# Two layers of fp32r matmuls on one core: finer start loads, spaced x loads, one seven-product quad fewer, and SBUF tiles at multiples of 512 bytes

## The chip, the cores and the metric

The kernel runs on one core of a Trainium2 chip. The time is the device time of one execution in microseconds; the figure of a kernel is the median of its runs. Before the change it is 2428.97 us (three runs, 2428.86 to 2429.07).

## The reference

A decoder trunk of two layers on 256 tokens of width 2048, in fp32. Layer 0 is a retention layer with 8 heads, layer 1 multi-head latent attention over a shared, compressed key and value; each is followed by an MLP with squared ReLU and 8192 hidden columns. The two MLPs hold most of the weights and are what the change mostly touches:

```
for layer in range(2):
    x = x + (retention if layer == 0 else mla)(rms_norm(x, norm_mix[layer]), ...)
    h = rms_norm(x, norm_mlp[layer])
    x = x + square(relu(h @ w1[layer])) @ w2[layer]     # 2048 -> 8192 -> 2048
```

## The kernel before, in words

**The product.** Every weight is read once, as fp32, by 1 MB loads on SyncE's (SP's) DMA queue into four `raw` buffers. A product of fp32 numbers is three fp32r matmuls: ScalarE (ACT) casts the high part `wh` of a weight, VectorE (DVE) subtracts it from `raw` and leaves the low part `wl` (`split`, L695), and TensorE (PE) does high by high, high by low and low by high. The last of these subtractions that was recorded is kept in `low_part[0]`.

**Quads.** The unit of the large products is `quad` (L826): two blocks of 128 rows of a weight by two of 512 columns, times both halves of the tokens. An ordinary quad has 8 products, 24 matmuls of 128x128 by 512 columns. A "seven" quad has 7 products, 21 matmuls, in Strassen's manner: DVE first makes sums of blocks of the weight (`u0`, `u1`; one addition over 1024 elements and two over 512), and four parts instead of two are split into `wh` and `wl`, seven half parts in place of four. `gemm_pair` (L882) does eight quads that sum into one set of PSUM banks; `kinds` says which of the eight are of the seven kind. L527 names sets of them: `SEVEN` (3, 5, 7), `LATE` (5, 7), `ODD` (1, 3, 5, 7).

**The MLP** (`mlp`, L1348) goes through the 8192 hidden columns in four groups. A group has two up pairs (p = 0 and 1 in the first group, to p = 6 and 7 in the last), which make eight hidden blocks, and then two down pairs, which use them. `u{layer}_{p}{quad}` names an up quad's tiles, `d{layer}_{group}{p}{quad}` a down quad's. A hidden block goes from PSUM through sums on DVE and ReLU on ACT, is cut into two 16-bit halves by copies (`hid_h`), turned by DMA transposes on SP's queue (`hid_t`, four for a half pair), copied together (`hid_u`), squared and split into `hid` on ACT and DVE, with sums `hid_more` for the seven quads. In profile names the numbers are left out: `u_wl`, `d_c`, `hid_t`.

**The residual stream** x lies in device memory (`xh`). At the end of each of four products (retention output, MLP 0, attention output, MLP 1) `x_tiles` (L622) brings it in: four blocks, two loads of 256 KB each, on GpSimd's (POOL's) queue. `later(n, f)` (L579) puts a step off by n quads, and `tick` (L587) counts them; so the code is recorded in an order in which, for example, block b of x is brought when 2b quads more have been recorded.

**The order of the work.** The engines do not run the code as recorded. `Plan` (L126) keeps every instruction as an `Op` with a table cost; `latest` (L256) goes backwards and gives each a due date; `forward` (L313) places them engine by engine, the earliest due date first among those that are ready by the plan; `schedule` (L293) repeats this six times and keeps the plan with the earliest end. `emit` (L469) writes the result out, so that nearly every instruction has the line L480 in the profile. Once written, each engine and each queue goes through its list strictly in order. `behind(op, other)` (L226) makes op wait for other. All SBUF tiles of a tag rotate through fixed slots; the first tiles of the program (`gains`, 448 bytes on each partition, `cst`, `inv`, 640 bytes) lie ahead of the pools of large tiles.

**The start.** `gemm_two` (L816) makes the first two projections (q and k of a head) together from `rq_raw`, half of which is loaded after the other, with the first loads of x transposed (`x0t`) between; `a0` is x times the norm's gain, one half of it by ACT and one by DVE. PE runs 11 idle matmuls on zeros until then.

Of the kernel before, what the change touches and what calls it, by code (L numbers as in the profile page):

```python
# [120 lines left out]
class Op:  # L121
    __slots__ = ("engine", "method", "args", "kw", "number", "before", "after", "cost", "took", "due", "start", "end",
                 "new", "left", "ready", "made", "held", "moves", "behind", "ahead")


class Plan:  # L126
# [19 lines left out]
    def record(self, engine, method, args, kw):  # L146
# [3 lines left out]
        op.made = op.held = None  # L150
# [105 lines left out]
    def latest(self):  # L256
# [4 lines left out]
        limit, free = {}, dict.fromkeys(self.LATENCY, 0.0)  # L261
# [8 lines left out]
        while True:  # L270
# [12 lines left out]
            op.due = free[e] = min(limit[op], free[e] - op.cost)  # L283
# [29 lines left out]
    def forward(self):  # L313
# [73 lines left out]
        while True:  # L387
            best = None
            for e in free:
                w, r = waiting[e], ready[e]  # L390
                while w and w[0][0] <= free[e]:
                    _, _, op = heapq.heappop(w)
                    heapq.heappush(r, (op.due, op.number, op))
# [11 lines left out]
            if not ready[e]:  # L405
                while waiting[e] and waiting[e][0][0] <= at:
                    _, _, op = heapq.heappop(waiting[e])
                    heapq.heappush(ready[e], (op.due, op.number, op))
# [102 lines left out]
P = 128  # L511
# [36 lines left out]
def yoco(ctx: ExitStack, tc: tile.TileContext, a):  # L548
# [48 lines left out]
    gains = nc.tile(pool, [P, G_ALL + 14], F32, "gains")  # L597
    cst = nc.tile(pool, [P, C_ALL - C_MASK], F32, "cst")
    inv = nc.tile(pool, [P, C_MASK], F32, "inv")
# [22 lines left out]
    def x_tiles(name):  # L622


        def bring(b):
            both = act_tile(f"x_{name}{b}", F32)
            for t in range(NT):
                x[t][b] = both[:, t].rearrange("p i s -> p (i s)")
                nc.gpsimd.dma_start(x[t][b], x_home[t][b])

        for b in range(NB):
            later(2 * b, lambda b=b: bring(b))
# [112 lines left out]
    def stream(w, chunk, cols, name, use, done=None, before=None):  # L745

        raw = nc.tile(pool, [P, 2048], F32, f"{name}_raw", "raw", 4)
        if before is None:
            nc.sync.dma_start(raw[:, :cols], w[chunk])
        n = cols // 2  # L750
        for half in range(2):
            wh = nc.tile(pool, [P, 1024], F32R, f"{name}_wh{half}", "wh", 5)
            wl = nc.tile(pool, [P, 1024], F32R, f"{name}_wl{half}", "wl", 5)
            cuts = 1
            if before is not None:
                cuts = 1 if half or chunk else 2
                m = n // cuts
                for i in range(cuts):
                    lo = half * n + i * m
                    nc.sync.dma_start(raw[:, lo : lo + m], w[chunk][:, lo : lo + m])  # L760
                    if i == 0:
                        before(half)
            m = n // cuts
            for i in range(cuts):
                lo = half * n + i * m
                low_part[0] = split(wh[:, i * m : (i + 1) * m], wl[:, i * m : (i + 1) * m], raw[:, lo : lo + m])
# [21 lines left out]
    def four_t(acc, act, k0, nk, wh, wl):  # L788

        for j in range(4):  # L790
# [25 lines left out]
    def gemm_two(w, act, nk, names, before, done):  # L816
# [3 lines left out]
        for g in range(n):  # L820
            stream(
                w, g, 2048, f"{names[0]}{g}", lambda half, wh, wl: four_t(acc[half], act, g * 4, nk, wh, wl),
# [989 lines left out]
```

## Time and profile before

| | |
|---|---|
| median of three runs | 2428.97 us (2428.86 to 2429.07) |
| the profiled execution, its time and its span | 2431.72 us, 2429.9 us |
| mean granted clock of TensorE | 0.996 |
| busy: PE, PEld, DVE, ACT, POOL | 2405.2, 2013.8, 2262.6, 1852.3, 219.2 us |
| their shares of the span | 99, 83, 93, 76, 9% |
| matmuls recorded | 11190 |
| bytes moved by DMA | 545.18 MB, 224 GB/s |

The profile shows one execution. PE are matmuls, PEld the loading of their stationary operand, DVE VectorE, ACT ScalarE, POOL GpSimd; SPq and POOLq are the DMA queues of SP and POOL. A row of a timeline has the start and the length in us, the engine, the operation with its tiles (out<-in, partitions x elements) and the count; in brackets stands how long the engine was idle before it, and what ended that. A row of the waits has engine and tile, what it waited for, and the total, the times and the longest in us. A group has busy time and mean ns of one, then the idle time before them. A row of a table by windows has the stretch, its length, and the busy time of PE, PEld, DVE, ACT and POOL with counts, then PEclk, the granted clock as a share of full speed, the busy share of the DMA engines, and GB/s. Times of one instruction from row to row are read from starts, since the ends of matmuls are modelled.

### The profile page before, as it was taken

To read this page: it belongs to the slowest core of one execution; us is meant where nothing else is said; L and a number is where in the kernel's file an instruction comes from. 1 tells how busy PE (TensorE), PEld (TensorE's weight loads), DVE (VectorE), ACT (ScalarE), POOL (GpSimd) and SP (SyncE) were. 2 spreads that over 40 slices of the span, in tenths; PEclk is the share of its full clock that TensorE was granted. 3 is DMA by queue.
4 is the path that set the end of the run, shared out by engine and by line. 5 is a ranking of instruction groups with operands and counts; after the bars stand their busy time and mean duration, and the time that the engine had idled before them with its cause. 6 is when DMAs were issued, how large, how long until landed. Compare 5 with 4: busy or idle time off the path is not lost. (4 is left out here: it accounts for less than half of the span.)

```text
span 2429.9 us, 31583 instructions
## 1 busy us (share of the span) xinstructions
PE 2405.2 (99%) x11190; PEld 2013.8 (83%) x11190; DVE 2262.6 (93%) x3002; ACT 1852.3 (76%) x2613; POOL 219.2 (9%) x245
## 2 busy tenths in 40 slices
PE   9999999999999999999999999999999999999999
PEld 7888888888887788888877888998887888888877
DVE  8999999989999999999989998877899999999989
ACT  7666766667787969769769979677879688697795
POOL 3000001011000010010110001110000100100100
PEclk9999999999999999999999999999999999999999
DMA  8566669667585698799897766545767997987974
GB/s 339 191 203 210 204 210 256 201 200 237 200 260 189 220 271 228 242 262 231 239 269 223 217 226 190 169 145 188 220 208 215 257 238 233 258 240 243 265 235 145
DMA packets 197136, 545.18 MB, mean 224 GB/s; under 512 B 115441, under 2 KB 116977, under 8 KB 143729
## 3 DMA queue, kind: packets, MB, share of 16 engines
q1 hardware_dynamic: 174720, 495.84, 63.5%
q0 software_dynamic: 21248, 46.15, 9.9%
q8 instruction: 87, 1.43, 0.2%
q10 hardware_dynamic: 1008, 1.18, 0.2%
q14 instruction: 73, 0.59, 0.1%
HBM read 478.09 MB, written 39.85 MB: 213 GB/s over the span
## 5 line engine op out<-in xcount | busy, mean ns | idle before, releaser
L480 PE MATMUL d_c<-d_wh,hid 128*128 128x512 f32 x1412 | 455.1, 391 | 4.2 <-ACT hid L480 4.2
L480 PE MATMUL u_c<-u_wh,n 128*128 128x512 f32 x1328 | 428.9, 390 | 3.1 <-ACT u_wh L480 3.1
L480 PEld LDWEIGHTS d_c<-d_wh,hid 128*128 128x128 f32 x1412 | 266.5, 189 | 61.4 <-ACT hid L480 5.0
L480 PEld LDWEIGHTS u_c<-u_wh,n 128*128 128x128 f32 x1328 | 249.7, 188 | 55.3 <-ACT u_wh L480 3.8
L480 DVE TENSOR_TENSOR d_wl<-d_raw,d_wh 128x1024 fp32r<-128x1024 f32 (+1 forms) x256 | 279.2, 1108 | 5.4 <-ACT d_wh L480 5.4
L480 ACT CAST u_wh<-u_raw 128x1024 fp32r<-128x1024 f32 (+1 forms) x256 | 235.9, 952 | 62.5 <-PE u_c L480 49.1
L480 DVE TENSOR_TENSOR u_wl<-u_raw,u_wh 128x1024 fp32r<-128x1024 f32 (+1 forms) x256 | 272.6, 1095 | 8.9 <-ACT u_wh L480 8.6
L480 PE MATMUL d_c<-d_wl,hid 128*128 128x512 f32 x706 | 275.8, 391 | 0.1
L480 ACT CAST d_wh<-d_raw 128x1024 fp32r<-128x1024 f32 (+1 forms) x256 | 240.4, 964 | 40.7 <-PE d_c L480 23.2
L480 PE MATMUL u_c<-u_wl,n 128*128 128x512 f32 x664 | 259.4, 391 | 3.1 <-DVE u_wl L480 3.1
L480 PE MATMUL rp_c<-rp_wh,a 128*128 128x512 f32 x640 | 206.6, 390 | 0.0
L480 ACT CAST rp_wh<-rp_raw 128x1024 fp32r<-128x1024 f32 (+1 forms) x128 | 118.4, 944 | 65.6 <-PE rp_c L480 36.7
L480 DVE TENSOR_TENSOR u_wl<-u_u,u_wh 128x1024 fp32r<-128x1024 f32 x120 | 145.3, 1220 | 22.3 <-ACT u_wh L480 21.6
L480 ACT CAST d_wh<-d_u 128x1024 fp32r<-128x1024 f32 x106 | 108.8, 1052 | 69.4 <-DVE d_u L480 59.6
L480 ACT CAST u_wh<-u_u 128x1024 fp32r<-128x1024 f32 x120 | 125.4, 1052 | 43.2 <-PE u_c L480 19.4
L480 PEld LDWEIGHTS d_c<-d_wl,hid 128*128 128x128 f32 x706 | 133.2, 189 | 28.2 <-DVE d_wl L480 0.5
L480 PEld LDWEIGHTS u_c<-u_wl,n 128*128 128x128 f32 x664 | 124.7, 188 | 32.4 <-DVE u_wl L480 6.6
L480 DVE TENSOR_TENSOR rp_wl<-rp_raw,rp_wh 128x1024 fp32r<-128x1024 f32 (+1 forms) x128 | 136.1, 1092 | 8.6 <-ACT rp_wh L480 7.8
L480 PEld LDWEIGHTS rp_c<-rp_wh,a 128*128 128x128 f32 x640 | 120.1, 188 | 26.0 <-DVE rk_u L480 0.9
L480 DVE TENSOR_TENSOR d_wl<-d_u,d_wh 128x1024 fp32r<-128x1024 f32 x106 | 127.6, 1220 | 5.9 <-ACT d_wh L480 5.6
L480 PE MATMUL u_p<-u_wh,n_more 128*128 128x512 f32 x360 | 122.7, 395 | 2.2 <-ACT u_wh L480 2.2
L480 PE MATMUL rp_c<-rp_wl,a 128*128 128x512 f32 x320 | 124.5, 389 | 0.0
(464 smaller groups left out, 5941.4 us busy)
## 6 DMA issues: line engine op xcount, KB each, us to landing
u_raw<-in_mlp_w SPq DMA_DIRECT2D x128, 1024.0 KB, 6.3
d_raw<-in_mlp_w SPq DMA_DIRECT2D x128, 1024.0 KB, 5.3
rp_raw<-in_ret_w_gv SPq DMA_DIRECT2D x64, 1024.0 KB, 5.0
ro_raw<-in_ret_w_out SPq DMA_DIRECT2D x32, 1024.0 KB, 5.1
uq_raw<-in_mla_w_uq SPq DMA_DIRECT2D x24, 768.0 KB, 4.2
rq_raw<-in_ret_w_qk SPq DMA_DIRECT2D x14, 1024.0 KB, 5.7
rk_raw<-in_ret_w_qk SPq DMA_DIRECT2D x14, 1024.0 KB, 5.3
xh<-d_c POOLq DMA_DIRECT2D x48, 256.0 KB, 5.5
```

The source lines that it names most:

```text
L480: op.made = fn(*(real(v) for v in op.args), **{k: real(v) for k, v in op.kw.items()})
```

## The change

There are four parts. (1) *Start:* the first group of the two first projections is loaded in four pieces of 512 columns, q and k by turns, and an op can carry a `first`, a place ahead of all due dates, which fixes the order of these loads and of the first x loads on SP; the cast of the positions goes from DVE to POOL. (2) *x loads and due dates:* `latest` lets the transfers of all queues share one server when it works out due dates, and each x load is recorded by itself, one per quad, from one quad later on, and waits for the last low-part subtraction recorded by then. (3) *Kinds of quads:* up pair p = 1 of both layers has the set (3, 5, 7) of seven quads in place of (1, 3, 5, 7): its quad 1 becomes ordinary. (4) *Addresses:* `gains` grows from 448 to 896 bytes per partition, and `inv` moves into a 2048-byte `f2k` slot. Before, the `raw` buffers began 64 bytes, and the other large tiles 192 bytes, past a multiple of 512; after, all begin at multiples of 512.

```diff
@@ -120,7 +120,7 @@
     __slots__ = ("engine", "method", "args", "kw", "number", "before", "after", "cost", "took", "due", "start", "end",
-                 "new", "left", "ready", "made", "held", "moves", "behind", "ahead")
+                 "new", "left", "ready", "made", "held", "moves", "behind", "ahead", "first")
@@ -147,7 +147,7 @@
         op.number, op.before, op.after, op.new = len(self.ops), {}, [], []
-        op.made = op.held = None
+        op.made = op.held = op.first = None
         op.behind, op.ahead = set(), []
@@ -258,7 +258,7 @@
         behind = {op: [] for op in self.ops}
-        limit, free = {}, dict.fromkeys(self.LATENCY, 0.0)
+        limit, free, server = {}, dict.fromkeys(self.LATENCY, 0.0), 0.0
         waiting = {e: [] for e in free}
@@ -280,7 +280,11 @@
             op = heapq.heappop(ready[e])[2] if ready[e] else heapq.heappop(waiting[e])[3]
-            op.due = free[e] = min(limit[op], free[e] - op.cost)
+            op.due = min(limit[op], free[e] - op.cost)
+            if op.moves is not None:
+                server = min(server, op.due + op.cost + op.moves[0]) - op.moves[0]
+                op.due = min(op.due, server - op.cost)
+            free[e] = op.due
             for other, finish in behind[op]:
@@ -390,7 +394,7 @@
                     _, _, op = heapq.heappop(w)
-                    heapq.heappush(r, (op.due, op.number, op))
+                    heapq.heappush(r, (op.due if op.first is None else op.first - 1e9, op.number, op))
                 at = free[e] if r else w[0][0] if w else None
@@ -405,7 +409,7 @@
                     _, _, op = heapq.heappop(waiting[e])
-                    heapq.heappush(ready[e], (op.due, op.number, op))
+                    heapq.heappush(ready[e], (op.due if op.first is None else op.first - 1e9, op.number, op))
             _, _, op = heapq.heappop(ready[e])
@@ -594,9 +598,9 @@
-    gains = nc.tile(pool, [P, G_ALL + 14], F32, "gains")
+    gains = nc.tile(pool, [P, G_ALL + 126], F32, "gains")
     cst = nc.tile(pool, [P, C_ALL - C_MASK], F32, "cst")
-    inv = nc.tile(pool, [P, C_MASK], F32, "inv")
+    inv = f2k([C_MASK], "inv")
     pos_i = nc.tile(few, [P, NT], I32, "pos_i")
@@ -626,10 +630,14 @@
                 x[t][b] = both[:, t].rearrange("p i s -> p (i s)")
-                nc.gpsimd.dma_start(x[t][b], x_home[t][b])
+                def load(dst=x[t][b], src=x_home[t][b]):
+                    nc.behind(nc.gpsimd.dma_start(dst, src), low_part[0])
+                later(t, load)
         for b in range(NB):
-            later(2 * b, lambda b=b: bring(b))
+            later(2 * b + 1, lambda b=b: bring(b))
@@ -742,28 +750,15 @@
-    def stream(w, chunk, cols, name, use, done=None, before=None):
+    def stream(w, chunk, cols, name, use, done=None):
         raw = nc.tile(pool, [P, 2048], F32, f"{name}_raw", "raw", 4)
-        if before is None:
-            nc.sync.dma_start(raw[:, :cols], w[chunk])
+        nc.sync.dma_start(raw[:, :cols], w[chunk])
         n = cols // 2
             wl = nc.tile(pool, [P, 1024], F32R, f"{name}_wl{half}", "wl", 5)
-            cuts = 1
-            if before is not None:
-                cuts = 1 if half or chunk else 2
-                m = n // cuts
-                for i in range(cuts):
-                    lo = half * n + i * m
-                    nc.sync.dma_start(raw[:, lo : lo + m], w[chunk][:, lo : lo + m])
-                    if i == 0:
-                        before(half)
-            m = n // cuts
-            for i in range(cuts):
-                lo = half * n + i * m
-                low_part[0] = split(wh[:, i * m : (i + 1) * m], wl[:, i * m : (i + 1) * m], raw[:, lo : lo + m])
+            low_part[0] = split(wh[:, :n], wl[:, :n], raw[:, half * n : half * n + n])
             use(half, wh, wl)
@@ -785,9 +780,9 @@
-    def four_t(acc, act, k0, nk, wh, wl):
-        for j in range(4):
+    def four_t(acc, act, k0, nk, wh, wl, js=range(4)):
+        for j in js:
             k = k0 + j
@@ -818,10 +813,28 @@
         for g in range(n):
-            stream(
-                w, g, 2048, f"{names[0]}{g}", lambda half, wh, wl: four_t(acc[half], act, g * 4, nk, wh, wl),
-                (lambda: done(acc)) if g == n - 1 else None, lambda half: before(g) if half == 0 else None,
-            )
+            raw = nc.tile(pool, [P, 2048], F32, f"{names[0]}{g}_raw", "raw", 4)
+            parts = [
+                [nc.tile(pool, [P, 1024], F32R, f"{names[0]}{g}_{i}{half}", i, 5) for i in ("wh", "wl")] for half in range(2)
+            ]
+            cuts = 1 if g else 2
+            m = 1024 // cuts
+            for i in range(cuts):
+                for half in range(2):
+                    lo = half * 1024 + i * m
+                    ins = nc.sync.dma_start(raw[:, lo : lo + m], w[g][:, lo : lo + m])
+                    if not g:
+                        ins.first = (0, 3, 4, 6)[2 * i + half]
+                    if half == i == 0:
+                        before(g)
+                    wh, wl = parts[half]
+                    low_part[0] = split(wh[:, i * m : (i + 1) * m], wl[:, i * m : (i + 1) * m], raw[:, lo : lo + m])
+            for i in range(cuts):
+                for half in range(2):
+                    four_t(acc[half], act, g * 4, nk, *parts[half], range(i * 4 // cuts, (i + 1) * 4 // cuts))
+            if g == n - 1:
+                queue.append((clock[0] + 0.5, -1, lambda: done(acc)))
+            tick()
@@ -1124,7 +1137,7 @@
     def first_tables():
-        nc.vector.tensor_copy(pos_f, pos_i)
+        nc.gpsimd.tensor_copy(pos_f, pos_i)
         turned_by.append(sincos(inv, C_MASK, "tab"))
@@ -1148,10 +1161,12 @@
         if c:
-            nc.sync.dma_start(t, a["xt"][:, 2 * c : 2 * c + 2, :])
+            ins = nc.sync.dma_start(t, a["xt"][:, 2 * c : 2 * c + 2, :])
+            if c == 1:
+                ins.first = 5
         else:
             for j in range(2):
-                nc.sync.dma_start(t[:, j], a["xt"][:, j, :])
+                nc.sync.dma_start(t[:, j], a["xt"][:, j, :]).first = 1 + j
         v = act_tile(f"a0_{c}")
@@ -1396,7 +1411,7 @@
             for p in range(f0 // 2, (f0 + nf) // 2):
-                seven = (ODD, ODD)[p % 2] if p else LATE
+                seven = (LATE, SEVEN, *(ODD, ODD) * 3)[p]
                 gemm_pair(
```

What the plan makes of it is shown at three places. First SP's list in layer 0, second up pair: `u0_16_raw` is the load of its quad 6, `hid0_00` the first hidden block pair of the first up pair (t0, t1 its two turned halves, h0 and h1 the 16-bit halves), `d0_000_raw` the first load of the down pair. Before:

```order
L480 DMA u0_15_raw_7116<-in_mlp_w1_0 128x2048
L480 DMA u0_17_raw_7197<-in_mlp_w1_0 128x2048
L480 DMA_TRANSPOSE hid0_00_t0_7212<-hid0_00_h0_7201 128x4x128
L480 DMA_TRANSPOSE hid0_00_t1_7222<-hid0_00_h0_7201 128x4x128
L480 DMA u0_16_raw_7236<-in_mlp_w1_0 128x2048
L480 DMA_TRANSPOSE hid0_00_t0_7212<-hid0_00_h1_7240 128x4x128
L480 DMA_TRANSPOSE hid0_00_t1_7222<-hid0_00_h1_7240 128x4x128
L480 DMA d0_000_raw_7291<-in_mlp_w2_0 128x2048
L480 DMA d0_001_raw_7312<-in_mlp_w2_0 128x2048
L480 DMA_TRANSPOSE hid0_01_t0_7374<-hid0_01_h0_7364 128x4x128
```

After, the same place:

```order
L484 DMA u0_15_raw_7143<-in_mlp_w1_0 128x2048
L484 DMA_TRANSPOSE hid0_00_t0_7166<-hid0_00_h0_7154 128x4x128
L484 DMA_TRANSPOSE hid0_00_t0_7166<-hid0_00_h1_7162 128x4x128
L484 DMA_TRANSPOSE hid0_00_t1_7189<-hid0_00_h0_7154 128x4x128
L484 DMA_TRANSPOSE hid0_00_t1_7189<-hid0_00_h1_7162 128x4x128
L484 DMA u0_17_raw_7211<-in_mlp_w1_0 128x2048
L484 DMA_TRANSPOSE hid0_01_t0_7217<-hid0_01_h0_7187 128x4x128
L484 DMA_TRANSPOSE hid0_01_t0_7217<-hid0_01_h1_7215 128x4x128
L484 DMA u0_16_raw_7239<-in_mlp_w1_0 128x2048
L484 DMA_TRANSPOSE hid0_01_t1_7243<-hid0_01_h0_7187 128x4x128
L484 DMA_TRANSPOSE hid0_01_t1_7243<-hid0_01_h1_7215 128x4x128
L484 DMA d0_000_raw_7310<-in_mlp_w2_0 128x2048
```

All four transposes of the first block pair now stand ahead of the load of quad 7, and those of the second ahead of the first load of the down pair.

Second, POOL's list at the x loads of MLP 0, with the semaphores that each load waits for (PE, DVE: that engine; DMASW: an earlier transfer of POOL's queue); `xh_0_1` is block 1 of x for the first half of the tokens. Before:

```order
L480 DMA x_mlp00_11555<-xh_0_0_455 128x512 [waits PE_49]
L480 DMA x_mlp00_11555<-xh_1_0_470 128x512
L480 DMA x_mlp01_11574<-xh_0_1_505 128x512 [waits PE_49]
L480 DMA x_mlp01_11574<-xh_1_1_514 128x512
L480 DMA x_mlp02_11590<-xh_0_2_525 128x512 [waits DMASW4_49,PE_49]
L480 DMA x_mlp02_11590<-xh_1_2_538 128x512 [waits DMASW5_49]
```

After:

```order
L484 DMA x_mlp00_11942<-xh_0_0_459 128x512 [waits DVE_49]
L484 DMA x_mlp00_11942<-xh_1_0_497 128x512 [waits DVE_49]
L484 DMA x_mlp01_12053<-xh_0_1_511 128x512 [waits DVE_49]
L484 DMA x_mlp01_12053<-xh_1_1_520 128x512 [waits DVE_49]
L484 DMA x_mlp02_12209<-xh_0_2_530 128x512 [waits DMASW4_49,DVE_49]
L484 DMA x_mlp02_12209<-xh_1_2_543 128x512 [waits DMASW5_49,DVE_49]
```

Each load waits for a subtraction of DVE of its own. The number at a tile's end counts what was recorded: the loads were recorded together, 11555 to 11668 with the fourth block, as the last up pair ended, and now stand apart, from 11942 on, beside the eight quads of the down pair after it.

Third, DVE's list at the start (`gqn` is a gain, `pos_f` the positions as floats, `rq00_wl` a low part of the first projections' weights, `a0_0` their other operand). Before:

```order
L480 TENSOR_SCALAR gqn_99<-gains_68 128x1
L480 CAST pos_f_111<-pos_i_78 128x2
L480 TENSOR_TENSOR rq00_wl0_118<-rq00_raw_74,rq00_wh0_108 128x512
L480 SCALAR_TENSOR_TENSOR a0_0_120<-x0t_0_80,gains_68,a0_0_120 128x256
L480 TENSOR_TENSOR rq00_wl0_118<-rq00_raw_74,rq00_wh0_108 128x512
L480 TENSOR_TENSOR rq00_wl1_155<-rq00_raw_74,rq00_wh1_148 128x1024
```

After:

```order
L484 TENSOR_SCALAR gqn_98<-gains_68 128x1
L484 TENSOR_TENSOR rq00_wl0_117<-rq00_raw_74,rq00_wh0_107 128x512
L484 SCALAR_TENSOR_TENSOR a0_0_119<-x0t_0_80,gains_68,a0_0_119 128x256 x2
L484 TENSOR_TENSOR rq00_wl1_144<-rq00_raw_74,rq00_wh1_132 128x512
L484 TENSOR_TENSOR rq00_wl0_117<-rq00_raw_74,rq00_wh0_107 128x512
```

The cast of the positions is gone from DVE, both halves of `a0` stand together, and the k half (`wl1`) comes between the two pieces of the q half.

## The prediction, on record before the changed kernel was run

> **What bounds the kernel now.** I read the page's first lines, then who TensorE (PE) waited for, then the stretches around those waits.
>
> ```profile
> span 2429.9 us, 31583 instructions
> PE 2405.2 (99%) x11190; PEld 2013.8 (83%) x11190; DVE 2262.6 (93%) x3002; ACT 1852.3 (76%) x2613; POOL 219.2 (9%) x245
> ```
>
> PE is busy 99% of the span: the floor is the matmuls themselves, and an edit can win only what PE waits, or a cheaper matmul. The waits of PE, all of them that matter here (us in total, times, longest):
>
> ```profile
> PE d_c L480 <- ACT hid L480: 4.2, 2, 2.4
> PE u_c L480 <- ACT u_wh L480: 3.1, 1, 3.1
> PE u_c L480 <- DVE u_wl L480: 3.1, 5, 0.8
> PE u_p L480 <- ACT u_wh L480: 2.2, 1, 2.2
> PE rq_acc L480 <- DVE a L480: 1.8, 1, 1.8
> PE u_p L480 <- DVE u_wl L480: 1.4, 2, 0.8
> ...
> PE d_c L480 <- DVE hid_more L480: 0.3, 1, 0.3
> PE rp_p L480 <- ACT rp_wh L480: 0.2, 1, 0.2
> ```
>
> They sit in three kinds of place: the start (rq_acc), the second up-projection pair of each layer and the down-projection after it, and the last up-projection pair of each layer. The same view cut to the second pair and what follows, in layer 0 (754 to 830 us) and in layer 1 (1795 to 1870 us), gives the shares:
>
> ```profile
> PE u_c L480 <- DVE u_wl L480: 0.7, 1, 0.7
> PE u_p L480 <- DVE u_wl L480: 0.6, 1, 0.6
> ```
> ```profile
> PE u_c L480 <- DVE u_wl L480: 1.4, 2, 0.8
> ```
>
> So VectorE (DVE) costs 0.7 + 0.6 + 1.4 = 2.7 us there, and the late hid block of ScalarE (ACT) 4.2, once per layer. Each longer stop also costs clock. Stretches after four of them (PE, PEld, DVE, ACT, POOL busy, then PEclk):
>
> ```profile
> 821.00:825.00 4.00, 4.00 (x12) 3.02 (x11) 3.81 (x6) 4.00 (x7) 0.00 (x0) 0.57 0.57 119
> 1275.00:1279.00 4.00, 3.83 (x9) 2.58 (x10) 3.03 (x5) 4.00 (x6) 0.00 (x0) 0.57 0.63 241
> 1862.00:1866.00 4.00, 3.92 (x10) 3.11 (x11) 3.91 (x8) 4.00 (x7) 0.00 (x0) 0.57 0.62 70
> 2316.00:2320.00 4.00, 4.00 (x11) 3.17 (x12) 3.97 (x5) 4.00 (x7) 0.00 (x0) 0.57 0.71 274
> ```
>
> A clock of 0.57 over 4 us loses 0.43 x 4 = 1.7 us, four times: 6.9 us. The Trainium skill (TensorE: Matmul & The Clock Gate, "HAM oscillation") puts the danger at PE gaps over about 3.4 us; here stops of 1.8, 2.2, 2.4 and 3.1 us each brought half clock, so the rows decide. By the page's rule none of the 6.9 us would hang on those stops, and the sum below would end 6.9 us higher, at 2421.
>
> Why the last up pair stops: POOL's x loads, SP's transposes and ACT in layer 1.
>
> ```profile
> 2288.85 3.57 POOL L480 DMA_DIRECT2D x_mlp<-xh  x6
> 2299.50 0.54 POOL L480 DMA_DIRECT2D x_mlp<-xh  x1 [7.08 <-PE u_c L480]
> ```
> ```profile
> 2297.53 7.71 SPq L480 DMA_TRANSPOSE hid_t<-hid_h  x4
> ```
> ```profile
> 2303.64 1.04 ACT L480 COPY hid_h<-u_c 128x1024 uint16<-128x1024 uint16 x1
> 2312.87 0.76 ACT L480 COPY hid_u<-hid_t 128x512 uint16<-128x512 uint16 x1 [8.19 <-DMA hid_t<-hid_h]
> ```
>
> Six x loads leave in 3.57 us, the transposes queue behind them, and ACT, in order, stands 8.19 us before the copy that needs a transpose, with u_wh casts behind it. Landing of the transposes in 2297 to 2317 us, and of those just after the pair (2342 to 2347 us):
>
> ```profile
> DMA to landing us min/median/max: 6.3/11.2/13.6
> ```
> ```profile
> DMA to landing us min/median/max: 2.4/2.4/5.2
> ```
>
> **The change part by part.** The profiled execution took 2431.7 us (span 2429.9); the median of the runs is 2428.97, 2.7 lower. The sum is made against 2431.7 and shifted by that. A run can tell about 0.2%, 4.9 us, from no change.
>
> *One seven-product quad fewer per layer* (pair 1, quad 1). It adds three matmuls per layer. Their price is the distance of starts at full clock, from these rows of PE (seven matmuls start from 825.62 up to 827.21):
>
> ```profile
> 822.47 0.63 PE L480 MATMUL d_c<-d_wl,hid 128*128 128x512 f32 x1
> ...
> 823.75 0.63 PE L480 MATMUL d_c<-d_wl,hid 128*128 128x512 f32 x1
> ...
> 825.62 0.39 PE L480 MATMUL d_c<-d_wl,hid 128*128 128x512 f32 x1
> ...
> 827.21 0.39 PE L480 MATMUL d_c<-d_wh,hid 128*128 128x512 f32 x1
> ```
>
> 1.59 / 7 = 0.227 us, so six matmuls add **1.4 us**, all on the path. DVE and ACT are relieved:
>
> ```profile
> L480 DVE TENSOR_TENSOR u_wl<-u_raw,u_wh 128x1024 fp32r<-128x1024 f32 x196 | 234.3, 1221 | 7.0 <-ACT u_wh L480 6.7
> L480 DVE TENSOR_TENSOR u_u<-u_raw 128x1024 f32<-128x1024 f32 x60 | 73.2, 1220 | 0.4
> L480 DVE TENSOR_TENSOR u_u<-u_u,u_raw 128x512 f32<-128x512 f32 x120 | 82.5, 687 | 1.0
> ```
>
> The sums go (1.22 + 2 x 0.69), and 3.5 low-part subtractions of 1.22 become two (1.9): 4.5 us of DVE per layer, and about 1.5 casts of ACT. In the same place SP's order puts the first hidden block's transposes ahead of the load of quad 7, so that ACT does that chain earlier. It has room early and none late (754 to 770, 797 to 818 us):
>
> ```profile
> 754.00:770.00 16.00, 16.00 (x72) 13.27 (x71) 14.11 (x22) 10.22 (x13) 5.10 (x1) 1.00 0.54 189
> 797.00:818.00 21.00, 21.00 (x94) 17.34 (x93) 19.10 (x28) 21.00 (x31) 0.00 (x0) 1.00 0.69 220
> ```
>
> ACT is busy 10.2 of 16 us, then 21 of 21. At stake are 2.7 (DVE) + 4.2 (hid) + 3.4 (two half-clock stretches) = 10.3 us. 4.5 us of DVE exceeds its 1.3 to 1.4 us of waits in either layer; the hid stop of 1.8 to 2.4 us meets some 1.6 us less ACT work plus the work moved earlier. I take 70%, **-7.2** (ends: -2.7, only the DVE waits; -10.3).
>
> *The x loads, one per quad, behind that quad's last DVE split.* They leave the last up pair and go to the down pair after it. At stake there: u_wh 3.1 + 2.2, the u_wl waits that follow, 0.8 twice (3.1 + 1.4 less the 2.7 above, less one of 0.3 elsewhere), and two half-clock stretches, 3.4: 5.3 + 1.5 + 3.4 = **-10.2**. Queued behind a waiting load on POOL stand only the other x loads and the write-back of x, which nothing waits for in that pair. Loads take this long:
>
> ```profile
> x_mlp<-xh POOLq DMA_DIRECT2D x16, 256.0 KB, 12.7
> ```
>
> Blocks 0 and 1 of x are wanted after the pair's eight quads, and their loads are tied to quads 0 to 3, about 20 us earlier, so 12.7 us are covered. What is late next: the transposes of the last hidden blocks now meet an x load each. PE already waited 0.3 us for hid_more at that place (1328 us), so there is no slack: **+2.5** for both layers together (ends 0, and the slower rival below). In the retention output and the attention output the same spacing applies; no row of PE's waits names x there, so nothing.
>
> *The start.* DVE stood in order behind a tiny table:
>
> ```profile
> 6.33 0.17 DVE L480 CAST pos_f<-pos_i 128x2 f32<-128x2 int32 x1 [1.70 <-DMA pos_i<-in_pos]
> ...
> 7.02 0.62 DVE L480 SCALAR_TENSOR_TENSOR a<-x0t,gains,a 128x256 fp32r<-128x256 f32 x1
> ```
> ```profile
> 4.80 0.51 ACT L480 ACTIVATE a<-x0t,gains 128x256 fp32r<-128x256 f32 x1
> ```
> ```profile
> 7.70 0.50 PE L480 MATMUL rq_acc<-a,rq_wh 128*128 128x512 f32 x1 [1.81 <-DVE a L480]
> ```
>
> pos_f goes to POOL, where only the angles that need it stand behind it. The operand is there from 5.3 us, so DVE could finish a at about 6.2 instead of 7.6, and PE start 1.5 us earlier. Cutting the second projection's first load in halves adds one DMA, one cast and one subtraction. From there to 74 us ACT and DVE feed PE closely (rp_wh, 0.2, is such a wait), so part is lost again: **-1.3** (ends: 0 and -3, the start's wait with the clock that goes with it).
>
> *The tiles' addresses.* Only gains and inv were not whole multiples of 512 bytes, so every other tile moves by one common amount: no two of them change place against each other. Where a cost per instruction hangs on the start address it is the rival below; otherwise 0. The new order of the rest swaps neighbours within a quad: 0.
>
> Sum: 1.4 - 7.2 - 10.2 + 2.5 - 1.3 = -14.8, 2431.7 to 2416.9 on the profile's scale, **2414** on that of the median.
>
> **The rivals.**
> *Given back.* ACT, full from 797 to 818 us, stays the limit: the hid stops remain (-2.7 instead of -7.2), the start gives nothing, and of the x gain 5 returns at the next hid wait beyond the 2.5: 1.4 - 2.7 - 10.2 + 2.5 + 5 = -4: 2425, within 0.2%. For it: ACT's 21 of 21. Against: its idle third from 754 on.
>
> *Slower: the collision moves with the loads.* The x loads now run beside the transposes of the last pair's two hidden blocks, in both layers, where PE has no slack. If each of these four sets is held up as today's were (11.2 against 2.4 us), each makes a stop like today's: 3.1 + 0.8 + 1.7 = 5.6, together 22.4 in place of the 2.5: 1.4 - 7.2 - 10.2 + 22.4 - 1.3 = +5.1, 2434; with the hid stops kept as well, 2441. It decides from about 4.3 us a stop, where the sum is zero. Against: one load per quad, not six in 3.57 us.
>
> *Cheaper matmuls.* At half clock the rows above give 1.28 / 3 = 0.427 us per matmul, so at full clock 0.2135 would be due; 0.227 is taken. Some 13 ns of every matmul do not follow the clock. If they come from operands that begin 192 bytes past a multiple of 512, all 11190 could lose them: 150 us of PE. DVE, 2262.6 busy and 9 less here, then binds: about 2300. For it: a cost that is nothing at half clock looks like reading, not multiplying. Against: every such tile has the same remainder now, so no row shows another case. The Trainium skill (TensorE: Matmul & The Clock Gate, "Back-to-back issue gap") has N/2.4 + 2.5 ns, 216 at 512 columns, for a matmul by itself, 11 ns under the row: by that estimate 123 us of PE. Its SBUF — State Buffer ("Door 1") speaks against this part of the change: lines of 16 bytes, and 192 is a whole number of those.
>
> **How the numbers follow.** Main case 0.58, own range 2405 to 2423 (its terms at their ends, less those of the rivals); given back 0.17 (2425); slower 0.13 (2434 to 2441); cheaper matmuls 0.12 (2300). Faster by over 0.2%: 0.58 + 0.12 = 0.70; within: 0.17; slower: 0.13. The range runs from 2404 to 2436: main, given back and half of the slower case, about 0.8; the cheap matmul stays out.
>
> **What would show it.** In the profile after: no ACT wait for hid_t and no PE wait for u_wh in the last up pair; PE clock 1.00 in all four places; PE's first real matmul near 6.2 us; hid waits of PE under 2 us in total; some 11196 matmuls still 0.227 us apart. PE waits for hid or hid_more in the down pair after the last up pair would show the slower rival; 0.216 or less between matmuls the cheap one. Wrong altogether would be the x loads still in one burst.

## The result, and the profile after

The changed kernel takes 2407.93 us (median of four runs, 2407.62 to 2409.0) beside 2429.02 us for the kernel before on the same chip: a ratio of 0.9913 (0.9896 to 0.9930), 21.1 us less. The forecast was 2414, 15 less, with a range from 2404 to 2436.

The first lines of the page after, then who TensorE waited for, all of it, then the granted clock:

```profile
span 2407.2 us, 31600 instructions
PE 2396.7 (100%) x11196; PEld 2011.0 (84%) x11196; DVE 2255.3 (94%) x2992; ACT 1849.2 (77%) x2610; POOL 226.7 (9%) x246
```
```profile
PE idle L484 <- DVE zeros L484: 1.2, 1, 1.2
PE u_c L484 <- DVE u_wl L484: 1.1, 2, 0.8
PE n_tp L484 <- ACT n2u L484: 1.0, 1, 1.0
PE rq_acc L484 <- ACT a L484: 0.7, 1, 0.7
PE rk_acc L484 <- DVE rq_wl L484: 0.7, 1, 0.7
PE u_p L484 <- DVE u_wl L484: 0.5, 1, 0.5
PE d_c L484 <- ACT u_c L484: 0.3, 2, 0.2
...
PE d_c L484 <- ACT hid_more L484: 0.2, 1, 0.2
```
```profile
core 0: 2407.2 us, clock 1.000
```

The waits for `hid` (4.2 us) and for `u_wh` (3.1 and 2.2) are gone, no wait is longer than 1.2 us, and the clock is whole. The matmuls are six more and cost what they did; seven of them still lie 1.59 us apart (825.61 to 827.20):

```profile
825.61 0.39 PE L484 MATMUL d_c<-d_wh,hid_more 128*128 128x512 f32 x1
...
827.20 0.39 PE L484 MATMUL d_p<-d_wh,hid_more 128*128 128x512 f32 x1
```

The same matmul of the program stands in both traces, so the difference of its starts, first matmul of a quad by first matmul, says where the time went:

```
first matmul of            before     after   after - before   step
first projections            7.70      5.99       -1.70
u0_0 (MLP 0)               710.42    710.06       -0.36       -0.4  start, retention
u0_1 (second up pair)      754.40    754.03       -0.37        0.0
d0_01                      842.40    839.43       -2.97       -2.6  second up pair and down pair, layer 0
u0_7 (last up pair)       1252.42   1250.76       -1.66       +1.3
d0_30                     1299.35   1291.55       -7.79       -6.1  last up pair, layer 0
u1_1                      1794.97   1786.33       -8.64       -0.9
d1_01                     1884.22   1869.29      -14.92       -6.3  second up pair and down pair, layer 1
u1_7                      2293.60   2278.75      -14.85       +0.1
d1_30                     2340.85   2319.55      -21.31       -6.5  last up pair, layer 1
end of the span            2429.9    2407.2       -22.7       -1.4
```

Four stretches carry 21.5 us, the four that the forecast had named. Each second pair also carries three added matmuls, 0.7 us, so its stops gave 3.3 and 7.0 us. Of the 1.3 us that come back between, 1.0 lie in `d0_10`: at 964.85, 984.87 and 1001.17 us TensorE falls 0.43, 0.11 and 0.48 us behind full pace, which it did not before; the first and the last follow waits for ACT.

The last up pair of layer 1 after, where the forecast showed six x loads in 3.57 us: the x loads on POOL in 2255 to 2370 us (durations, then first and last start), the transposes on SP, their landing in 2278 to 2312 us, and ACT's first copy of a turned half:

```profile
L484 POOL DMA_DIRECT2D x_mlp<-xh x8: 538/538/575, 2317.2 to 2358.9; - x8
```
```profile
2280.95 8.12 SPq L484 DMA_TRANSPOSE hid_t<-hid_h  x5
```
```profile
DMA to landing us min/median/max: 2.3/4.0/6.2
```
```profile
2294.86 0.78 ACT L484 COPY hid_u<-hid_t 128x512 uint16<-128x512 uint16 x1
```

Two things changed at once: the loads are gone from here, and the copy stands 13.9 us behind the first transpose (2294.86 less 2280.95) where it was reached 7.15 us behind it before (2312.87 less 8.19 of waiting, less 2297.53). Which of the two counts, the rows cannot say.

### The profile page after: what moved, and what is told of

It reads as the page before. It is cut to its first block, busy times and chain, and to the rows that moved or that the text cites. A ratio compares the mean times of both kernels' runs of the same rounds, so it can differ in the third digit from the quotient of the medians.

```text
span 2407.2 us, 31600 instructions
## 1 busy us (share of the span) xinstructions
PE 2396.7 (100%) x11196; PEld 2011.0 (84%) x11196; DVE 2255.3 (94%) x2992; ACT 1849.2 (77%) x2610; POOL 226.7 (9%) x246
## 4 chain that ended last, share of the span: by engine, by line
PE 58%; DVE 5%; ACT 3%; issue 2%; DMA 1%; POOL 0%; SPq 0%; DVEq 0%; ACTq 0%; POOLq 0%
PE d_c L484 17%; PE u_c L484 16%; PE u_p L484 5%; PE d_p L484 5%; PE uq_acc L484 4%; PE wo_acc L484 2%; PE ku_acc L484 2%; DVE d_wl L484 2%; PE dqp_c L484 1%; PE wop_c L484 1%; PE dq_acc L484 1%; DVE u_wl L484 1%; PE s L484 1%; PE kd_acc L484 1%; DVE d_u L484 1%
## 5 line engine op out<-in xcount | busy, mean ns | idle before, releaser
L484 PE MATMUL u_c<-u_wh,n 128*128 128x512 f32 x1352 | 434.8, 389 | 0.0
L484 PE MATMUL u_p<-u_wh,n_more 128*128 128x512 f32 x348 | 116.5, 389 | 0.0
```

The source lines that it names most:

```text
L484: op.made = fn(*(real(v) for v in op.args), **{k: real(v) for k, v in op.kw.items()})
```

## The experiments

The theory at the outset was that of the prediction: the time is in TensorE's stops and the half clock behind them; the ordinary quad removes those of the second up pair and the spaced x loads those of the last one. Its rivals were the addresses, and the new due dates by themselves. Since the kernel before moved between 2429.0 and 2430.7 from one set of runs to the next, each result is given against the kernel before in its own set of runs: the time, the ratio with its interval, and the difference in us. The changed kernel stands at -21.1 on that scale; differences of 1 or 2 us on it tell nothing.

**Addresses, both ways.** The first edit is to the changed kernel, the second to the kernel before; neither alters any engine's instructions or their order.

```diff
-    gains = nc.tile(pool, [P, G_ALL + 126], F32, "gains")
+    gains = nc.tile(pool, [P, G_ALL + 126 + 48], F32, "gains")
```

> The changed kernel with gains wider by another 192 bytes: every instruction in the same order, but all large tiles begin 192 bytes past a multiple of 512 again, as they did before the change. Theory of the stops (the time comes from waits of TensorE and their half clock, addresses are worth nothing): 2407.9, within 2 us, matmuls of 512 columns still 0.227 us apart. Rival, the addresses (tiles at multiples of 512 are read or written faster by some engine or transfer): 5 us or more slower, 2413 or above, since the measured gain of 21 us passed the forecast of 15 by about that much.

```diff
-    gains = nc.tile(pool, [P, G_ALL + 14], F32, "gains")
+    gains = nc.tile(pool, [P, G_ALL + 126], F32, "gains")
...
-    inv = nc.tile(pool, [P, C_MASK], F32, "inv")
+    inv = f2k([C_MASK], "inv")
```

> The kernel before with the addresses alone changed (gains 896 bytes wide, inv in an f2k slot): all engines' instructions in the same order, all large tiles at multiples of 512. Theory of the stops: 2429.0, within 2 us, with the same waits of TensorE. Rival, the addresses: 2424 or below.

Measured: 2407.77 (0.9907, 0.9893 to 0.9920; -22.9) and 2428.09 (0.9986, 0.9977 to 0.9995; -2.6). In the changed program the addresses are worth nothing that can be told. The second kernel is 2.6 us better than its neighbour, less than the rival wanted, with the same waits for hid (4.2 us); in its profile the stops of the last up pair are cut up otherwise, and the two stretches of half clock behind them are not there. Whether the addresses did that or the chance of an execution is not settled: the kernel before alone ran from 2425.9 to 2433.9 in that set. The eleven executions of the second kernel fall into two groups, three of 2422.9 to 2424.0 us with a granted clock of 1.000 and eight of 2427.2 to 2429.4 with 0.996 to 0.999, so what differs goes with the clock.

The addresses in the two programs are a little other than was said above. Before, only one of the four `raw` buffers began 64 bytes past a multiple of 512, the other three 192; and the second edit moves that buffer by 448 bytes but most other large tiles by 1856, so the tiles do not all keep their distance from each other there. The first edit moves all large tiles alike, by 192.

**The ordinary quad: taken out of the changed kernel, and alone on the kernel before.**

```diff
-                seven = (LATE, SEVEN, *(ODD, ODD) * 3)[p]
+                seven = (LATE, ODD, *(ODD, ODD) * 3)[p]
```

> The changed kernel with the second up pair of both layers back at quads 1, 3, 5, 7 of the seven kind; all else as changed. The matmuls fall by six (1.4 us). Theory: the ordinary quad's relief of VectorE and ScalarE is what ended the stops in the second pair and in the down pair after it; they return, some 9 to 10 us less 1.4: 2415 to 2417. Rival: the due dates with the shared server, which set SP's transposes ahead of the load of quad 7 in this kernel too, ended them: then this is faster by the matmuls, 2406.5.

```diff
-                seven = (ODD, ODD)[p % 2] if p else LATE
+                seven = (LATE, SEVEN, *(ODD, ODD) * 3)[p]
```

> The kernel before with one edit alone, quads 3, 5, 7 of the seven kind in the second up pair. Theory: it takes away the stops of the second up pair and the down pair after it with their half clock, 10.3 us as in the profile after, and adds 1.4 us of matmuls; the last up pair's stops stay: 8.9 below the kernel before. Rival: here too the new due dates are needed: within 2 us of the kernel before.

Measured: 2415.87 (0.9941, 0.9927 to 0.9954; -14.8, so 6 to 8 us worse than the changed kernel) and 2420.57 (0.9961, 0.9946 to 0.9975; -9.6). The waits of TensorE, longest part, without the quad and with it alone:

```profile
PE u_c L484 <- DVE u_wl L484: 3.3, 5, 0.8
PE d_c L484 <- ACT hid L484: 2.4, 1, 2.4
```
```profile
PE u_c L480 <- ACT u_wh L480: 3.9, 2, 2.9
...
PE d_c L480 <- ACT hid L480: 0.2, 1, 0.2
```

The second pair's stops (`u_wl`, `hid`) return without it; with it alone they go and the last pair's (`u_wh`) stay. The theory holds for this half. One `hid` stop, that of layer 0, does not return, nor is it there with the due dates alone, below. The waits for DVE in layer 0's second pair show the two edits against each other: 1.3 us before, 0.4 with the quad alone, 1.9 with the due dates alone or without the quad, and 1.3 again in the changed kernel (0.8 and 0.5).

**The x loads as before, in the changed kernel.**

```diff
-                def load(dst=x[t][b], src=x_home[t][b]):
-                    nc.behind(nc.gpsimd.dma_start(dst, src), low_part[0])
-                later(t, load)
+                nc.gpsimd.dma_start(x[t][b], x_home[t][b])
...
-            later(2 * b + 1, lambda b=b: bring(b))
+            later(2 * b, lambda b=b: bring(b))
```

> The changed kernel with the x loads as before the change (both halves of a block together, one block per two quads, no wait on a subtraction); all else as changed. Theory: their burst holds up the transposes of the last up pair, and the 6.1 and 6.5 us that the profile after shows as gained in the last up pair of the two layers go again: 2420, with waits of TensorE for u_wh there. Rival: the due dates with the shared server ended those stops by themselves: 2408.

Measured: 2407.27 (0.9907, 0.9892 to 0.9920; -23.4), no stop in the last pair. The theory failed here: in the changed kernel the spacing is not needed. The loads left earlier and less closely (2272.0 to 2288.1 us), so this run did not yet say why.

**The due dates as before; the spacing alone.** The first takes the shared server out of the changed kernel, the second is the kernel before with the spacing only (the edit above, the other way round).

```diff
-            op.due = min(limit[op], free[e] - op.cost)
-            if op.moves is not None:
-                server = min(server, op.due + op.cost + op.moves[0]) - op.moves[0]
-                op.due = min(op.due, server - op.cost)
-            free[e] = op.due
+            op.due = free[e] = min(limit[op], free[e] - op.cost)
```

> The changed kernel with due dates worked out as before, without the shared server for transfers; the x loads still one per quad, each behind a subtraction. Theory after the run with the x loads as before: either of the two edits keeps the x loads away from the transposes of the last up pair, so the spacing alone is enough: 2408, within 2 us. Rival: the due dates, through the order of the transposes and of ScalarE's copies, ended these stops, and the spacing is worth nothing: 2418 to 2421, with waits of TensorE for u_wh in the last up pair.

> The kernel before with one edit alone, the x loads one per quad, each behind a subtraction. Theory: the stops of the last up pair go in both layers, 12.6 us as in the profile after, those of the second pair stay: 12 to 13 below the kernel before. Rival, the spacing is worth nothing without the due dates: within 2 us of the kernel before.

Measured: 2412.4 (0.9927, 0.9910 to 0.9943; -17.8) and 2418.14 (0.9952, 0.9937 to 0.9967; -12.0). The spacing alone removes the last pair's stops, as the prediction said. But in the changed kernel without the shared server new ones come behind them:

```profile
PE n_tp L480 <- DVE n L480: 2.7, 1, 2.7
PE d_c L480 <- ACT hid L480: 1.8, 1, 1.8
PE d_c L480 <- ACT hid_more L480: 1.7, 1, 1.7
```
```profile
1386.80:1390.20 3.40, 3.40 (x15) 3.40 (x16) 2.91 (x7) 2.45 (x6) 0.88 (x1) 0.50 0.53 141
```

They are in the down pair after the last up pair, in both layers, and in the normalisation after layer 0's, with a stretch of half clock. So neither the theory (2408) nor its rival (2418 to 2421) came out. The down pair is the place of the slower rival of the prediction, and the two layers have different causes. In layer 0 it is held-up transposes, as that rival had it: the last pair, issued at 1305.2 and 1306.4 us with an x load at 1306.0 between, landed after 10.1 and 9.2 us (3.5 and 2.9 in the changed kernel), ACT stood 3.04 us before the copy that needs them, and TensorE stopped 1.7 us at 1318.1 us:

```profile
DMA to landing us min/median/max: 9.2/9.7/10.1
```
```profile
1315.27 1.39 ACT L480 COPY hid_u<-hid_t 128x512 uint16<-128x512 uint16 x2 [3.04 <-DMA hid_t<-hid_h]
```

In layer 1 it is not: the slowest transpose of 2255 to 2370 us landed after 7.0 us, in the changed kernel after 8.8. There SP issued the last pair at 2344.25 us, 21.3 us after the first matmul of `d_30` (2322.97), and in the changed kernel at 2335.91, 16.4 us after it (2319.55). So the old due dates had put the last hidden block 5 us later. Why TensorE stops in the normalisation stays open.

**The start as before, in the changed kernel** (`gemm_two`, `first_inputs` and the cast of the positions as they were).

```diff
-        nc.gpsimd.tensor_copy(pos_f, pos_i)
+        nc.vector.tensor_copy(pos_f, pos_i)
...
-                    if not g:
-                        ins.first = (0, 3, 4, 6)[2 * i + half]
```

> The changed kernel with the start as before the change (first loads, their order, the cast of the positions on VectorE). By the profile after, the gain of 1.7 us at TensorE's first real matmul has shrunk to 0.4 us after the first projections: 0.4 us slower, 2408.3. Rival, the forecast's 1.3 with the clock that goes with it: 2409.2 or above.

Measured: 2408.97 (0.9914, 0.9900 to 0.9929; -21.2): 1.0 us slower by the times, nothing by the differences to the kernel before, so what the new start is worth cannot be told from nothing.

**A burst, with the new due dates.** All eight x loads leave together, ahead of the transposes of the last up pair.

```diff
             for p in range(f0 // 2, (f0 + nf) // 2):
+                if p == 7:
+                    x_tiles(f"mlp{layer}", True)
...
-            if last:
-                x_tiles(f"mlp{layer}")
...
-                later(t, load)
+                load() if together else later(t, load)
...
-            later(2 * b + 1, lambda b=b: bring(b))
+            later(1 if together else 2 * b + 1, lambda b=b: bring(b))
```

> The changed kernel, due dates with the shared server and all, but with the eight x loads of each MLP leaving together behind the last subtraction of the first quad of the last up pair, some 5 us ahead of the transposes there. Theory: a burst of x loads beside the transposes is what makes the stops, whatever the due dates: the transposes take 10 us and more to land, TensorE waits in the last up pair of both layers, and most of the 12.6 us gained there goes again: 2418 to 2421. Rival: in this order of the work there is room for late transposes, and a burst costs under 3 us: 2411 or below.

Measured: 2408.48 (0.9907, 0.9892 to 0.9922; -21.7). The burst was there, the transposes were late, and nobody waited. POOL's loads in 2260 to 2325 us, the first transposes, their landing, and ACT's copy:

```profile
L484 POOL DMA_DIRECT2D x_mlp<-xh x8: 536/537/575, 2274.8 to 2281.8; - x8
```
```profile
2280.01 11.97 SPq L484 DMA_TRANSPOSE hid_t<-hid_h  x5
```
```profile
DMA to landing us min/median/max: 3.6/7.0/12.3
```
```profile
2296.91 0.78 ACT L484 COPY hid_u<-hid_t 128x512 uint16<-128x512 uint16 x1
```

12.3 us at the worst, twice the 6.2 of the changed kernel, but the copy stands 16.9 us behind the first transpose, with no idle time before it. So the theory was mended: the stop needs both, transposes held up by a burst and a copy set closer behind them in ACT's order than they take. In this run the copy also stood 3 us further behind than in the changed kernel, but 12.3 us is less than the 13.9 there too.

**The due dates alone, on the kernel before** (the diff of the shared server, the other way round).

> The kernel before with one edit alone: due dates with the shared server. Theory after the burst run (the stops of the last up pair need both late transposes and a copy of ScalarE set close behind them): the x loads still leave together, but ScalarE's copies stand further behind the transposes, so TensorE does not wait for u_wh in the last up pair; those stops go, 12 us, and the second pair's stay: 2417 to 2419 beside 2430 for the kernel before. Rival: the burst still makes ScalarE wait here, since the other edits gave it the room: within 3 us of the kernel before.

Measured: 2425.48 (0.9983, 0.9974 to 0.9992; -4.1), a third of what the theory expected and just more than the rival allowed. One layer did what the mended theory said, the other did not. First layer 0, then layer 1: the first transposes, their landing, the copy:

```profile
1254.05 15.12 SPq L484 DMA_TRANSPOSE hid_t<-hid_h  x6
```
```profile
DMA to landing us min/median/max: 5.2/10.1/16.4
```
```profile
1272.34 1.38 ACT L484 COPY hid_u<-hid_t 128x512 uint16<-128x512 uint16 x2 [8.21 <-DMA hid_t<-hid_h]
```
```profile
2295.78 10.49 SPq L484 DMA_TRANSPOSE hid_t<-hid_h  x6
```
```profile
DMA to landing us min/median/max: 5.3/7.0/8.6
```
```profile
2306.20 1.41 ACT L484 COPY hid_u<-hid_t 128x512 uint16<-128x512 uint16 x2 [0.34 <-DMA hid_t<-hid_h]
```

The due dates put the copy 10.1 us behind the first transpose in both layers (1272.34 less 8.21 less 1254.05; 2306.20 less 0.34 less 2295.78). In layer 0 the eight loads left within 11.3 us and a transpose took 16.4, and TensorE stopped for 5.0 us; in layer 1 they left over 16.2 us, the slowest took 8.6, and it did not stop. Seven kernels side by side, layer 0 and layer 1 of each, in us:

```
kernel                        copy behind first transpose   slowest landing   ACT's wait
before                              8.1    7.15               13.5   13.6      7.1   8.2
before, tiles at multiples of 512   8.1    7.15               11.6   10.2      5.6   5.0
quads 3, 5, 7 alone                 7.15   7.15               13.3   11.4      8.0   6.0
spacing alone                       8.0    7.15                6.1    7.5      0     0.5
due dates alone                    10.1   10.1                16.4    8.6      8.2   0.3
changed                            13.6   13.9                 7.3    6.2      0     0
changed, x loads in a burst        16.9   16.9                11.0   12.3      0     0
```

In the seven places where the slowest landing passes the distance by 3 us or more, ACT waits 5.0 to 8.2 us; in the seven others 0.5 us at most. The seven other kernels fit: their slowest landing is 8.3 us, no distance is under 7.15, and ACT waits 0.75 us at most. The table also shows that the due dates alone widen the distance to 10.1 us only; it is 10.0 in the changed kernel without the ordinary quad (9.98 and 9.99), so the quad adds the rest.

**Two edits at places that still wait.**

```diff
-                seven = (LATE, SEVEN, *(ODD, ODD) * 3)[p]
+                seven = (LATE, SEVEN if layer else LATE, *(ODD, ODD) * 3)[p]
...
-QUERY, FOUR = (3, 4, 6, 7), (3, 5, 6, 7)
+QUERY, FOUR = (3, 4, 6, 7), (2, 3, 4, 5, 6, 7)
```

> The changed kernel with two edits at places where its profile still shows room: the second up pair of layer 0 has quads 5 and 7 of the seven kind (quad 3 becomes ordinary: 0.7 us of matmuls for the two stops of 1.0 and 0.7 us there), and the attention output's paired product has quads 2, 3, 4, 5, 6, 7 of the seven kind in place of 3, 5, 6, 7, where VectorE is busy 42 of 60 us (two quads, 1.4 us of matmuls less). Theory: 1.0 and 1.4 us less, 2405.5. Rival: the sums that the two new seven quads need come late, and the stops that this makes give the gain back: 2408 or above.

> The changed kernel with the first of those two edits alone (layer 0, second up pair, quads 5 and 7 of the seven kind). Theory: the two stops of 1.0 and 0.7 us go for 0.7 us of matmuls: 2406.9. Rival: one of the stops stays or the work behind it becomes late, as with every new plan: 2408 or above.

Measured: 2414.89 with both (0.9936, 0.9924 to 0.9949) and 2406.25 with the first alone (0.9899, 0.9886 to 0.9913; -23.9). The first removes the waits at 775 and 786 us; it is the fastest of all, though its interval overlaps the changed kernel's. The second failed by new waits in that product, of ACT's casts above all:

```profile
PE wop_c L484 <- ACT wop_wh L484: 3.2, 4, 1.0
PE wop_p L484 <- DVE wop_wl L484: 1.5, 3, 0.6
```

The forecast of the second edit had read the wrong stretch. The 60 us in which DVE is busy 42 are the product before the paired one, which runs from 1701 to 1742 us; two rows of the changed kernel (stretch and length, busy times of PE, PEld, DVE, ACT and POOL):

```profile
1640.00:1700.00 60.00, 60.00 (x326) 51.75 (x325) 41.78 (x78) 42.70 (x85) 6.56 (x10) 1.00 0.53 184
1700.00:1742.00 42.00, 42.00 (x187) 34.62 (x186) 35.85 (x42) 35.62 (x55) 1.08 (x2) 1.00 0.77 227
```

In the paired product itself DVE and ACT are each busy 85% of the time, and two more seven quads load both.

## Why the prediction was right, point by point

The direction and the four places were right, the cause of the last pair's stops only by half. The sum was short: 14.8 us on the scale of the profiles, where 22.7 came (21.1 by the medians), so that the result, 2407.9, lies near the lower end of the main case's own range, 2405 to 2423. The terms:

- **What bounds it.** Right: TensorE's stops and their half clock were all there was to win, and 21.5 of the 22.7 us of the span came from the four stretches named.
- **Six matmuls, +1.4.** Right: 0.227 us apart as before.
- **The second up pair, -7.2.** Right for the late hidden blocks and for layer 1, mis-sized: 3.3 and 7.0 us by the stages, 10.3 together, the end of its range; 11.0 when the quad is alone (9.6 and the 1.4 of the matmuls). That the sum of the two layers equals what was at stake is luck. In layer 0 the waits for DVE stayed, 1.3 us before and after, though 4.5 us less work was to end them: the due dates took back what the quad gave there. Layer 1 gave more than its waits and half clock as listed (5.5), because a stop costs more than the idle time in the list: the two for hid, 1.79 and 2.39 us there, set the matmuls back by 2.06 and 2.66 us by their starts (820.22 and 1862.08 us). The 70% was too careful: ACT's windows of 754 to 770 and 797 to 818 us had 10.2 and 21.0 us of work before and have 12.0 and 20.9 after. It is still full in the second, but more of the chain is done by then.
- **The x loads, -10.2.** Right in place and about in size: 12.6 us by the stages, 12.0 for the spacing alone. Incomplete in its cause: the step looked at the loads and not at the distance of ACT's copy, which the due dates and the ordinary quad together nearly double; with it the loads of before the change cost nothing either.
- **The new wait, +2.5.** This term failed: the stretches from `d0_30` and from `d1_30` on gave nothing back (-0.9 and -1.4). The wait itself is real in another order of the work: in the changed kernel without the shared server TensorE stops for 1.7 and 1.8 us there, in layer 0 for the reason forecast, held-up transposes, in layer 1 for another, a hidden block planned late. The new due dates end both, and the working gave this edit no term of its own. (In the slower rival, 2441 does not fit the -2.7 that the other rival takes for kept hid stops; with that it would be 2439.)
- **The start, -1.3.** TensorE begins 1.7 us earlier, as worked out at 1.5; 0.8 is left when the next product begins (33.01 before, 32.18 after), since waits of 0.7 and 0.7 us and shorter ones follow at once, and 0.4 when MLP 0 does. The half clock from 8.98 to 12.40 us that the kernel before has there is gone, and is in these figures.
- **Addresses, 0.** Right for the changed program, though the tiles do not move by one common amount, as the step had it. The cheaper matmul is refuted: 0.227 us at a remainder of 0 as at one of 192 bytes, and the same time. The lines of 16 bytes of the Trainium skill (SBUF — State Buffer, "Door 1") fit that, since 192 is a whole number of them. Where the 13 ns that do not follow the clock come from stays open.
- **The clock, 6.9.** Right in sum, since none of the four stretches of half clock is left, but the rule behind it, that each such stop brings one, is too simple (last section). Without the ordinary quad the changed kernel has the 2.4 us stop for hid and, in its trace, no half clock behind it.

## What to carry to other kernels

The stop of an engine that works in order needed two things here, a transfer that came late and an instruction set close behind it; measure the distance between issue and use beside the slowest landing, since either can be mended, and an edit that only mends one may owe its success to the other. When a scheduler's costs change together with the code, give the scheduler a term and an experiment of its own. A stop of TensorE can cost clock as well, some 1.7 us a stretch here, so one of 2 to 3 us may be much dearer than its length. And when the busy share of an engine is to show room for an edit, the window must be that of the product that is edited.

## What the runs showed of the hardware

Stretches of half clock lie on a grid of 3.413 us within one execution: in the kernel before they begin at 8.98, 821.36, 1275.33, 1862.42 and 2316.39 us, which are 238, 133, 172 and 133 steps apart, and each is one step long. What decides is how much of one step TensorE stood still. Two such steps of the kernel before, each with the step behind it, then three of the changed kernel without the ordinary quad, then two of the kernel with the spacing alone (stretch and length, busy times of PE, PEld, DVE, ACT and POOL, then PEclk):

```profile
817.94:821.36 3.42, 1.63 (x8) 0.93 (x6) 3.38 (x6) 3.42 (x6) 0.00 (x0) 1.00 0.39 77
821.36:824.77 3.41, 3.41 (x10) 2.64 (x9) 3.23 (x5) 3.41 (x6) 0.00 (x0) 0.50 0.60 118
1859.01:1862.42 3.41, 1.02 (x5) 0.51 (x4) 3.35 (x5) 3.41 (x6) 0.00 (x0) 1.00 0.39 77
1862.42:1865.84 3.42, 3.42 (x10) 2.65 (x9) 3.35 (x6) 3.42 (x6) 0.00 (x0) 0.50 0.71 81
```
```profile
1850.04:1853.45 3.41, 2.31 (x10) 1.36 (x8) 3.41 (x4) 3.41 (x5) 0.00 (x0) 1.00 0.29 89
1853.45:1856.86 3.41, 2.11 (x9) 1.65 (x10) 3.27 (x7) 3.41 (x6) 0.00 (x0) 1.00 0.42 94
1856.86:1860.27 3.41, 3.41 (x17) 2.80 (x16) 3.41 (x5) 3.41 (x7) 0.00 (x0) 1.00 1.07 168
```
```profile
819.17:822.58 3.41, 1.63 (x8) 1.22 (x8) 3.38 (x5) 3.41 (x6) 0.00 (x0) 1.00 0.53 104
822.58:826.00 3.42, 3.42 (x17) 2.81 (x16) 3.23 (x6) 3.42 (x6) 0.00 (x0) 1.00 0.62 141
```

With TensorE busy 1.02 of 3.41 us the next step is at half clock; with 2.11 it is not, though that stop, 2.40 us of waiting for hid, is the one of 2.38 us that cost half clock in the kernel before: it fell across two steps. At 1.63 it went once one way and once the other. In the fourteen traces together, of the steps that began at full clock, all twelve with 1.52 us of busy time or less were followed by half clock, none with 1.90 or more, and three of the eleven between. That the window runs free and is 3413 ns long is also in the Trainium skill (TensorE: Matmul & The Clock Gate, "What's actually happening"), and the grid agrees; its limit for stops, over about 3.4 us ("HAM oscillation"), does not: stops of 1.8 to 3.1 us were enough here. So the same program can pay for a stop in one execution and not in the next, which fits the wider scatter of the kernel before (2425.9 to 2433.9 in 15 runs; the changed kernel 2407.6 to 2409.0 in four). The granted clock of each execution bears this out: in the 46 executions of the kernel before that stand beside the experiments, the six with a mean clock of 0.999 took 2427.7 us on average, the 30 with 0.998 or 0.997 took 2429.9, and the ten with 0.996 or less 2431.5. No run changed the place of the grid alone.
